# The operands of the two branch products made in two parts under attention, kept in DRAM, and only loaded in the branch stage

## The chip, the cores and the metric

The kernel runs on one core of a Trainium2 chip. The metric is the device time of one execution in microseconds (us): 3035.47 us is the median of three runs of the kernel before, which lie between 3035.05 and 3037.78. The engines are TensorE (PE), VectorE (DVE), ScalarE (ACT), GpSimd (POOL) and SyncE (SP). SP does nothing but issue transfers between DRAM and the on-chip memory; POOL issues some as well, on a queue of its own.

## The reference

One layer of a streaming encoder is computed for a prompt of 512 tokens and a sample of 64 tokens, T = 576 columns in all, with a model width of 2048. Cut to what matters here:

```python
proj = h @ w_in                                   # all projections of the layer
o_a, S_new = gated_delta_rule(q, k, v, g, beta, S0)
o_a = rmsnorm(o_a, gdn_norm_w) * silu(z_a)        # (T, 16 heads x 128)
y_a = o_a @ w_branch_a                            # first branch product, 2048 x 2048
o_b = sparse_attention(...)                       # 16 heads, top-k of the keys
y_b = (o_b * silu(z_b)) @ w_branch_b              # second branch product, 2048 x 2048
merged = sigmoid(gl_a) * y_a + sigmoid(gl_b) * y_b
x = x + gate * (merged @ w_out)                   # third product, then a last rmsnorm
```

The operand of the first branch product is called ga in the kernel (o_a times silu(z_a)), that of the second gb.

## The kernel before, in words

**Tiles.** All large products run as a stream of 189 tiles. A tile is one block of 128 columns of a weight matrix against all 2048 rows and all 576 tokens. A float32 product is made out of three reduced-precision products: the weight is split into two parts (whi, wlo) and the activation as well (hi and lo), and whi x hi, whi x lo and wlo x hi are summed. So a tile is 96 matmuls of 288 columns: 64 with whi (part 0), then 32 with wlo (part 1). `run_tile` (L314) issues them. While tile n runs, `split` (L276) makes the parts of tile n+1's weight: ACT copies four quarters of the raw weight to whi and their negative to wlo, and POOL then adds the raw weight onto wlo with two accumulating transfers. At the 84th matmul `load` lets SP fetch the raw weight of tile n+3. The same splitting of an activation is the helper `two` (L253): ACT writes the high part, DVE subtracts it to make the low part.

**Stages around the change.** Attention runs under the tiles of the query and of the gate z_b, two tiles to a head, with `attend` (L1344) for the prompt and `attend_sample` (L1397) for a pair of heads of the sample; its result is the gated tile gb of a head, stored to DRAM as `d_gb`. Before attention, the delta rule has stored its heads to `d_oa`, and silu(z_a) of heads 0 to 11 to `d_za`. Heads 12 to 15 of z_a are tiles of their own behind attention (za12 to za15, tiles 129 to 132 of the stream). Then come eight tiles of the gate of branch b (g18 to g115, tiles 133 to 140), 16 tiles of the first branch product (ya, tiles 141 to 156), 16 of the second (yb) and 16 of the output product (wo).

`open_ga` (L1789) stands in front of tile 133. It ends attention, frees its memory, lays the two parts of ga there and starts `load_ga` (L1562), which fetches half a head of d_oa and d_za at a time, multiplies on DVE and splits with `two`, in 32 steps under the eight gate tiles. `open_branch` (L1799), in front of the first ya tile, does the same for gb with `load_gb` (L1599), in 16 steps under the ya tiles.

**What sets the order.** Work beside the tiles is written as tasks (generators). After each matmul the builder looks which tasks are due by its own estimate of the engines' clocks (`tick`, L156), and has them issue their next instructions at that place of the program. That is done when the program is built. On the chip each engine works through its own list strictly in that order, and an instruction whose operand isn't there holds all that stand behind it on that engine. A stage boundary runs every task to its end before it goes on:

```python
    def drain(self):
        while self.tasks:
            self.join(*self.tasks)

    def open_ga(self):
        self.drain()
        self.c3.close()
```

`join` moves the builder's own clock on to the next due time without a matmul in between, so whatever tasks still have to issue then stands in one piece in front of the tile, on every engine's list.

Of the kernel before, what the change touches and what calls it, by code (L numbers as in the profile page):

```python
# [7 lines left out]
F32 = mybir.dt.float32  # L8
F32R = mybir.dt.float32r
I32 = mybir.dt.int32  # L10
AF = mybir.ActivationFunctionType
ALU = mybir.AluOpType
# [8 lines left out]
T = 576  # L21
# [6 lines left out]
H = 16  # L28
# [180 lines left out]
class Kern(Plan):  # L209
# [138 lines left out]
    def consts(self, ctx):  # L348
        nc, tc, i = self.nc, self.tc, self.i
        cp = self.cp = ctx.enter_context(tc.tile_pool(name="cp", bufs=1))  # L350
        self.ident = cp.tile([128, 128], F32, name="ident")
        self.A.dma_start(self.ident, i["k_ident"])
        self.mE = cp.tile([128, 2, 128], F32, name="mE")
        self.ones = cp.tile([128, 1], F32, name="ones")
        self.V.memset(self.ones, 1.0)
        self.pm = ctx.enter_context(tc.tile_pool(name="pm", bufs=3, space=PSUM))
        self.px = ctx.enter_context(tc.tile_pool(name="px", bufs=2, space=PSUM))
        self.pc = ctx.enter_context(tc.tile_pool(name="pc", bufs=2, space=PSUM))
        self.po = ctx.enter_context(tc.tile_pool(name="po", bufs=1, space=PSUM))
        self.dp = ctx.enter_context(tc.tile_pool(name="dp", bufs=1, space=DRAM))  # L360
        dt = self.dp.tile
        self.d_g = dt([16, TX], F32, name="d_g")
        self.d_kT = dt([2, 128, T], F32, name="d_kT")
        self.d_v = dt([T, 256], F32, name="d_v")
        self.d_oa = dt([H, 128, T], F32, name="d_oa")
        self.d_za = dt([H, 128, T], F32, name="d_za")
        self.d_gb = dt([H, 128, T], F32, name="d_gb")
        self.d_t = dt([2, KO, 128, T], F32, name="d_t")
        self.d_ya = dt([KO, 128, T], F32, name="d_ya")
        self.d_f = dt([16, 384], F32, name="d_f")  # L370
        self.d_F = dt([16, 128, 384], F32, name="d_F")
        self.d_D = [dt([128, T], F32, name=f"d_D{e}") for e in range(2)]
# [971 lines left out]
    def attend(self, a):  # L1344
        S, p, h = self.S, self.p3, a["h"]
        yield from self.wait(self.kv_task)
        BT = p.tile([128, 256], F32, tag="BT", name=f"BT{h}")
        S.dma_start(BT, self.toeplitz(h, 128, 256))
        yield [BT, a["qT"], a["zt"]]
        yield from self.wait(*[self.spawn(self.attend_block(a, t, BT)) for t in (3, 2, 1, 0)])  # L1350
        if h % 2:
            a["sample"] = self.spawn(self.attend_sample(h // 2))

# [43 lines left out]
    def attend_sample(self, m):  # L1397
        V, A, S, p = self.V, self.A, self.S, self.p3
        KT, KC, VV = self.kvs
        sc = 128 ** -0.5  # L1400
        at = [self.att[2 * m], self.att[2 * m + 1]]
# [7 lines left out]
        for g, (k, n, n0) in enumerate(((KC[:, 0:512], 512, 512), (KC[:, 512:1024], 512, 384), (KT[:, TP:T], 64, 0))):  # L1409
            pl = yield from self.tp(f"lgs{m}{g}")  # L1410
            self.mm(pl[:, :n], qs, k)
            a = 512 * g
# [9 lines left out]
        for g in range(3):  # L1422
            n = 4 if g < 2 else 1
# [14 lines left out]
        for s in range(2):  # L1438
            gb = at[s]["gb"]
            V.scalar_tensor_tensor(gb[:, TP:], po[:, 64 * s:64 * s + 64], 0.5, at[s]["zt"][:, TP:], op0=ALU.mult, op1=ALU.mult)  # L1440
        self.drop("po")
        yield [at[0]["gb"], at[1]["gb"]]
        for s in range(2):
            S.dma_start(self.d_gb[2 * m + s], at[s]["gb"])

    def qb_pre(self, h):
        def pre():
# [33 lines left out]
    def zb_epi(self, h):  # L1481
        def epi(ps, s):
            p, a = self.p3, self.att[h]
            if s == 0:
                a["zt"] = p.tile([128, T], F32, tag="zt", name=f"zt{h}", bufs=4)
            self.silu2(ps, s, a["zt"])
            if s == 1:
                if h >= 3:
                    t = self.att[(h - 3) | 1]
                    self.join(t["task"])  # L1490
                    self.join(t["sample"])
                a["gb"] = p.tile([128, T], F32, tag="gb", name=f"gb{h}", bufs=3)
                a["task"] = self.spawn(self.attend(a))
        return epi
# [65 lines left out]
        return epi  # L1560

    def load_ga(self):  # L1562
        units = [(h, s) for h in range(H) for s in range(2)]
        t = {}

        def load(n):
            if n < len(units):
                h, s = units[n]
                t[n] = [self.p5.tile([128, 288], F32, tag=g, name=f"{g}{n}", bufs=3) for g in ("oa", "za")]
                for x, d in zip(t[n], (self.d_oa, self.d_za)):  # L1570
                    self.S.dma_start(x, d[h][:, 288 * s:288 * s + 288])
        load(0)
        load(1)
        for n, (h, s) in enumerate(units):
            load(n + 2)
            o, z = t.pop(n)
            yield [o, z]
            self.V.tensor_tensor(o, o, z, op=ALU.mult)
            yield [o]
            sl = slice(288 * s, 288 * s + 288)  # L1580
            self.two(o, self.ga[0][:, h, sl], self.ga[1][:, h, sl])

    def ya_pre(self, j):
        def pre():
# [13 lines left out]

    def load_gb(self):  # L1599
        for h in range(H):  # L1600
            t = self.p6.tile([128, T], F32, tag="gbl", name=f"gbl{h}")
            self.S.dma_start(t, self.d_gb[h])
            yield [t]
            self.two(t, self.gb[0][:, h, :], self.gb[1][:, h, :])
            yield 4000

    def yb_pre(self, j):
        def pre():
# [170 lines left out]
    def open_att(self):  # L1779
        self.drain()  # L1780
        self.c2.close()
        self.c3, self.p3 = self.pool("p3")
        self.slack = 0.0
        self.gpool = lambda: self.p3
        self.spawn(self.conv_out())
        self.spawn(self.gate_vectors())
        self.qb_pre(0)()

    def open_ga(self):  # L1789
# [152 lines left out]
```

## Time and profile before

| | |
|---|---|
| median of three runs | 3035.47 us |
| profiled execution: time, span | 3037.4 us, 3035.6 us |
| PE, PE weight load busy | 2938.0 us (97%), 2824.9 us (93%) |
| ACT, DVE, POOL busy | 1531.8 us (50%), 1205.0 us (40%), 399.3 us (13%) |
| bytes moved | 558.84 MB, mean 184 GB/s |

The profiled execution took 3037.4 us; the span from its first to its last instruction is 3035.6 us, and all places in the trace are counted from the span's start. Busy time of PE is an overlap of pipelined matmuls, each about 300 ns long and started every 0.13 us; a stretch in which PE is busy throughout runs at the pace of its matmuls, and what is missing there is time in which PE waited.

### The profile page before, as it was taken

What the parts mean: (1) busy time and instruction counts of PE and PEld (TensorE: products, weight loads), DVE (VectorE), ACT (ScalarE), POOL (GpSimd) and SP (SyncE); (2) the same over time, 40 slices, a digit from 0 to 9 for tenths busy, and PEclk for the clock granted to TensorE, in tenths of its full rate; (3) what the DMA queues carried; (4) which work ended last, traced back from release to release, by engine and by line L of the source; (5) the groups of instructions that cost most, each with busy time, mean ns of one, the idle gap of its engine ahead of it and who ended that gap; (6) DMA issues with size and microseconds to landing.
All of it is one profiled execution on the core that took longest, in us unless ns stands there. A gap on an engine that the chain in (4) does not pass through costs nothing.

```text
span 3035.6 us, 59288 instructions
## 1 busy us (share of the span) xinstructions
PE 2938.0 (97%) x23931; PEld 2824.9 (93%) x23931; DVE 1205.0 (40%) x3643; ACT 1531.8 (50%) x3428; POOL 399.3 (13%) x792
## 2 busy tenths in 40 slices
PE   5999999999999999999999999899999999999897
PEld 2599999999999999999999999899999999999897
DVE  3344896544454455544542434244322111112112
ACT  3266445555555555655554545354544443344454
POOL 1011111111111111111111111000111111111110
PEclk7999999999999999999999999999999999999999
DMA  9875887667677666767768677777679889888875
GB/s 326 273 162 125 188 191 183 158 161 177 154 164 168 157 161 155 172 163 173 168 158 191 164 165 179 177 168 167 151 171 263 231 223 225 217 204 213 217 160 139
DMA packets 571379, 558.84 MB, mean 184 GB/s; under 512 B 55121, under 2 KB 465650, under 8 KB 569890
## 3 DMA queue, kind: packets, MB, share of 16 engines
q1 hardware_dynamic: 515794, 354.69, 40.8%
q0 software_dynamic: 55168, 200.30, 34.5%
q8 instruction: 188, 3.08, 0.4%
q14 instruction: 85, 0.70, 0.1%
q10 hardware_dynamic: 144, 0.07, 0.0%
HBM read 313.52 MB, written 47.48 MB: 119 GB/s over the span
## 4 chain that ended last, share of the span: by engine, by line
PE 82%; DMA 10%; ACT 3%; DVE 2%; SPq 2%; issue 1%; POOL 0%; ACTq 0%; DVEq 0%; POOLq 0%
PE mm L221 66%; DMA yl<-d_ya 2%; SPq L58 2%; DMA za<-d_za 2%; DMA wlo<-wraw 1%; DMA wa<-in_w_ada 1%; DMA gbl<-d_gb 1%; PE ob L221 1%; PE lg L221 1%; PE ada L221 1%; PE po L221 1%; PE mmp L221 1%; PE dot L221 1%; DMA xf<-in_x_sample 1%; ACT wlo L58 1%
## 5 line engine op out<-in xcount | busy, mean ns | idle before, releaser
L221 PE MATMUL mm<-hh,whi 128*128 128x288 f32 (+1 forms) x4448 | 1223.8, 301 | 3.9 <-ACT gth L58 3.7
L221 PE MATMUL mm<-hl,whi 128*128 128x288 f32 (+1 forms) x4448 | 1221.2, 300 | 0.0
L221 PEld LDWEIGHTS mm<-hh,whi 128*128 128x128 f32 (+1 forms) x4448 | 838.0, 188 | 13.8 <-ACT gth L58 4.2
L221 PEld LDWEIGHTS mm<-hl,whi 128*128 128x128 f32 (+1 forms) x4448 | 838.4, 188 | 8.2 <-issue 3.8
L221 PE MATMUL mm<-hh,wlo 128*128 128x288 f32 (+1 forms) x4448 | 685.1, 302 | 0.0
L221 PEld LDWEIGHTS mm<-hh,wlo 128*128 128x128 f32 (+1 forms) x4448 | 615.4, 189 | 1.9 <-issue 0.9
L58 POOL DMA_DIRECT2D wlo<-wraw x376 | 323.2, 860 | 2231.9 <-ACT wlo L58 1875.4
L58 ACT ACTIVATE whi<-wraw 128x512 fp32r<-128x512 f32 x756 | 467.3, 618 | 96.9 <-DMA wraw<-in_w_branch_b 61.0
L58 ACT ACTIVATE wlo<-whi 128x512 fp32r<-128x512 f32 x752 | 475.2, 632 | 77.2 <-PE mm L221 37.3
L221 PE MATMUL mm<-ga,whi 128*128 128x288 f32 x1024 | 141.9, 299 | 8.2 <-DVE ta L58 8.2
L221 PEld LDWEIGHTS mm<-ga,whi 128*128 128x128 f32 x1024 | 139.5, 191 | 8.9 <-DVE ta L58 8.9
L221 PE MATMUL mm<-mg,whi 128*128 128x288 f32 x1024 | 144.0, 298 | 0.0
L221 PE MATMUL mm<-gb,whi 128*128 128x288 f32 x1024 | 139.9, 296 | 0.6 <-DVE tb L58 0.6
L221 PEld LDWEIGHTS mm<-mg,whi 128*128 128x128 f32 x1024 | 138.7, 189 | 0.0
L221 PEld LDWEIGHTS mm<-gb,whi 128*128 128x128 f32 x1024 | 137.5, 188 | 1.3 <-DVE tb L58 1.3
L58 DVE SCALAR_TENSOR_TENSOR cv<-raw,cw,cv 128x579 f32<-128x579 f32 x144 | 117.9, 818 | 27.8 <-ACT cv L58 24.2
L58 DVE SCALAR_TENSOR_TENSOR gacc<-gada,cs,gacc 128x512 f32<-128x512 f32 x120 | 86.2, 744 | 3.2 <-DMA gada<-in_w_ada 3.2
L58 ACT ACTIVATE raw<-mm 128x288 f32<-128x288 f32 x96 | 36.7, 382 | 82.9 <-PE mm L221 82.1
L58 ACT ACTIVATE gth<-mm 128x288 f32<-128x288 f32 x64 | 25.9, 407 | 103.7 <-PE mm L221 102.5
L58 ACT ACTIVATE x<-px 128x128 f32<-128x128 f32 x80 | 21.9, 273 | 107.7 <-PE px L221 107.7
L58 DVE TENSOR_TENSOR xf<-yp,xf 128x512 f32<-128x512 f32 (+1 forms) x18 | 11.4, 632 | 161.7 <-PE yp L236 134.0
L58 DVE SCALAR_TENSOR_TENSOR tb<-tb,mm 128x288 f32<-128x288 f32 x32 | 14.5, 453 | 144.3 <-DMA tb<-d_t 105.1
(494 smaller groups left out, 3437.8 us busy)
## 6 DMA issues: line engine op xcount, KB each, us to landing
wlo<-wraw POOLq DMA_DIRECT2D x376, 512.0 KB, 5.4
wraw<-in_w_in SPq DMA_DIRECT2D x140, 1024.0 KB
wa<-in_w_ada SPq DMA_DIRECT2D x64, 512.0 KB
gada<-in_w_ada SPq DMA_DIRECT2D x64, 256.0 KB
wraw<-in_w_branch_a SPq DMA_DIRECT2D x16, 1024.0 KB
wraw<-in_w_branch_b SPq DMA_DIRECT2D x16, 1024.0 KB
wraw<-in_w_out SPq DMA_DIRECT2D x16, 1024.0 KB
d_t<-gth SPq DMA_DIRECT2D x32, 288.0 KB
```

What stands on the lines that cost most here:

```text
L58: r = f(*a, **k)
L221: self.nc.tensor.matmul(out, lhsT, rhs, start=start, stop=stop, **k)
```

## The change

In attention, each head's gb is now split into its two parts in three pieces of 192 columns: `part` copies the high part on ACT, subtracts on DVE and stores both with SP. Two pieces hold columns of the prompt alone, the third is made when the sample is done. A new task, `ga_parts`, started when attention begins, goes through all 16 heads in three pieces each: SP loads 192 columns of d_oa and d_za, DVE multiplies, and `part` splits and stores. Every piece, of ga or gb, goes through one pair of buffers (shi, slo), and a piece of ga through one pair of load buffers (so, sz); `part` holds the pair until 3000 ns of the builder's clock after its stores. DRAM now keeps two parts of each operand, `d_ga` and `d_gb`. In the branch stages `load_ga` and `load_gb` only load the parts into the on-chip operands, 32 transfers of 288 KB each, issued by POOL.

```diff
--- before.py
+++ after.py
@@ -364,7 +364,7 @@
         self.d_v = dt([T, 256], F32, name="d_v")
         self.d_oa = dt([H, 128, T], F32, name="d_oa")
         self.d_za = dt([H, 128, T], F32, name="d_za")
-        self.d_gb = dt([H, 128, T], F32, name="d_gb")
+        self.d_ga, self.d_gb = (dt([2, H, 128, T], F32, name=n) for n in ("d_ga", "d_gb"))
         self.d_t = dt([2, KO, 128, T], F32, name="d_t")
         self.d_ya = dt([KO, 128, T], F32, name="d_ya")
         self.d_f = dt([16, 384], F32, name="d_f")
@@ -1348,6 +1348,7 @@
         S.dma_start(BT, self.toeplitz(h, 128, 256))
         yield [BT, a["qT"], a["zt"]]
         yield from self.wait(*[self.spawn(self.attend_block(a, t, BT)) for t in (3, 2, 1, 0)])
+        a["split"] = [self.spawn(self.part(a["gb"], self.d_gb, h, s)) for s in range(2)]
         if h % 2:
             a["sample"] = self.spawn(self.attend_sample(h // 2))
 
@@ -1439,9 +1440,34 @@
             gb = at[s]["gb"]
             V.scalar_tensor_tensor(gb[:, TP:], po[:, 64 * s:64 * s + 64], 0.5, at[s]["zt"][:, TP:], op0=ALU.mult, op1=ALU.mult)
         self.drop("po")
-        yield [at[0]["gb"], at[1]["gb"]]
         for s in range(2):
-            S.dma_start(self.d_gb[2 * m + s], at[s]["gb"])
+            at[s]["split"].append(self.spawn(self.part(at[s]["gb"], self.d_gb, 2 * m + s, 2)))
+
+    def part(self, src, dst, h, s):
+
+        p, c = self.p3, slice(192 * s, 192 * s + 192)
+        yield [src]
+        yield from self.take("part")
+        hi, lo = (p.tile([128, 192], F32R, tag=n, name=f"{n}{dst.tensor.name}{h}{s}", bufs=1) for n in ("shi", "slo"))
+        self.two(src if src.shape[1] == 192 else src[:, c], hi, lo)
+        yield [hi, lo]
+        self.S.dma_start(dst[0, h][:, c], hi.bitcast(F32))
+        self.S.dma_start(dst[1, h][:, c], lo.bitcast(F32))
+        yield 3000
+        self.drop("part")
+
+    def ga_parts(self):
+
+        p = self.p3
+        for h in range(H):
+            for s in range(3):
+                o, z = (p.tile([128, 192], F32, tag=n, name=f"{n}{h}{s}", bufs=1) for n in ("so", "sz"))
+                c = slice(192 * s, 192 * s + 192)
+                self.S.dma_start(o, self.d_oa[h][:, c])
+                self.S.dma_start(z, self.d_za[h][:, c])
+                yield [o, z], 3000
+                self.V.tensor_tensor(o, o, z, op=ALU.mult)
+                yield from self.part(o, self.d_ga, h, s)
 
     def qb_pre(self, h):
         def pre():
@@ -1489,6 +1515,7 @@
                     t = self.att[(h - 3) | 1]
                     self.join(t["task"])
                     self.join(t["sample"])
+                    self.join(*self.att[h - 3]["split"])
                 a["gb"] = p.tile([128, T], F32, tag="gb", name=f"gb{h}", bufs=3)
                 a["task"] = self.spawn(self.attend(a))
         return epi
@@ -1560,25 +1587,10 @@
         return epi
 
     def load_ga(self):
-        units = [(h, s) for h in range(H) for s in range(2)]
-        t = {}
-
-        def load(n):
-            if n < len(units):
-                h, s = units[n]
-                t[n] = [self.p5.tile([128, 288], F32, tag=g, name=f"{g}{n}", bufs=3) for g in ("oa", "za")]
-                for x, d in zip(t[n], (self.d_oa, self.d_za)):
-                    self.S.dma_start(x, d[h][:, 288 * s:288 * s + 288])
-        load(0)
-        load(1)
-        for n, (h, s) in enumerate(units):
-            load(n + 2)
-            o, z = t.pop(n)
-            yield [o, z]
-            self.V.tensor_tensor(o, o, z, op=ALU.mult)
-            yield [o]
-            sl = slice(288 * s, 288 * s + 288)
-            self.two(o, self.ga[0][:, h, sl], self.ga[1][:, h, sl])
+        for h in range(H):
+            for s in range(2):
+                self.G.dma_start(self.ga[s][:, h, :], self.d_ga[s, h])
+            yield 2000
 
     def ya_pre(self, j):
         def pre():
@@ -1598,11 +1610,9 @@
 
     def load_gb(self):
         for h in range(H):
-            t = self.p6.tile([128, T], F32, tag="gbl", name=f"gbl{h}")
-            self.S.dma_start(t, self.d_gb[h])
-            yield [t]
-            self.two(t, self.gb[0][:, h, :], self.gb[1][:, h, :])
-            yield 4000
+            for s in range(2):
+                self.G.dma_start(self.gb[s][:, h, :], self.d_gb[s, h])
+            yield 8000
 
     def yb_pre(self, j):
         def pre():
@@ -1784,6 +1794,7 @@
         self.gpool = lambda: self.p3
         self.spawn(self.conv_out())
         self.spawn(self.gate_vectors())
+        self.spawn(self.ga_parts())
         self.qb_pre(0)()
 
     def open_ga(self):
```

How the change moves instructions is shown at two places of the program. The first is the boundary between tile 132 (za15) and the gate tiles. On ACT, before, the four quarters of the weight of tile 134 stand right behind the two copies that end za15; whi and wlo are the parts of a weight, gz is z_a's gate, mm a tile's sum, gth a gate tile's result, and the number behind a name is the tile's or the head's:

```order
L58 ACTIVATE gz15_26606<-mm132_0_26511 128x288
L58 ACTIVATE gz15_26606<-mm132_1_26554 128x288
L58 ACTIVATE whi134_26657<-wraw134_26495 128x512
L58 ACTIVATE wlo134_26658<-whi134_26657 128x512
...
L58 ACTIVATE wlo134_26658<-whi134_26657 128x512
L58 ACTIVATE ga0_26635<-oa0_26642 128x288
L58 ACTIVATE gth18_26754<-mm133_0_26640 128x288
```

On ACT now (shid_ga_84 is the buffer of a high part of ga; the digits behind it are the head and the piece, so 110 is head 11, piece 0):

```order
L58 ACTIVATE gz15_27235<-mm132_0_27128 128x288
L58 ACTIVATE gz15_27235<-mm132_1_27181 128x288
L58 ACTIVATE shid_ga_84102_27259<-so102_27167 128x192
L58 ACTIVATE shid_ga_84110_27271<-so110_27266 128x192
L58 ACTIVATE shid_ga_84111_27282<-so111_27277 128x192
...
L58 ACTIVATE shid_ga_84151_27414<-so151_27409 128x192
L58 ACTIVATE shid_ga_84152_27425<-so152_27420 128x192
L58 ACTIVATE whi134_27448<-wraw134_27108 128x512
L58 ACTIVATE wlo134_27449<-whi134_27448 128x512
...
L58 ACTIVATE gth18_27545<-mm133_0_27441 128x288
```

Sixteen copies of ga pieces (head 10's last, then heads 11 to 15 with three each) now stand between za15 and the weight of tile 134; the ten rows left out are pieces of heads 12 to 14 and the rest of heads 11 and 15, and the other gap holds six more quarters of the weight.

On SP, at the same place, before (oa and za are the halves of a head that load_ga fetches):

```order
L58 DMA wraw135_26613<-in_w_in 128x16x128
L58 DMA d_za_83<-gz15_26606 128x576
L58 DMA oa0_26642<-d_oa_82 128x288
L58 DMA za0_26643<-d_za_83 128x288
L58 DMA oa1_26646<-d_oa_82 128x288
L58 DMA za1_26647<-d_za_83 128x288
...
L58 DMA wraw136_26767<-in_w_in 128x16x128
```

On SP now (so and sz are the loads of a ga piece, d_ga its stores, wraw a raw weight):

```order
L58 DMA wraw135_27242<-in_w_in 128x16x128
L58 DMA d_za_83<-gz15_27235 128x576
L58 DMA d_ga_84<-shid_ga_84102_27259 128x192
L58 DMA d_ga_84<-slod_ga_84102_27260 128x192
L58 DMA so110_27266<-d_oa_82 128x192
L58 DMA sz110_27267<-d_za_83 128x192
L58 DMA d_ga_84<-shid_ga_84110_27271 128x192
L58 DMA d_ga_84<-slod_ga_84110_27272 128x192
L58 DMA so111_27277<-d_oa_82 128x192
...
L58 DMA d_ga_84<-slod_ga_84152_27426 128x192
L58 DMA wraw136_27551<-in_w_in 128x16x128
```

Each piece of ga is four rows in a fixed order, load, load, store, store. The fetch of the raw weight of tile 136 stood behind five pairs of loads, and now stands behind all pieces up to head 15.

The second place is POOL's list under the gate tiles. Before, it holds the two accumulating transfers of each tile's weight and nothing else:

```order
L58 DMA wlo133_26517<-wraw133_26343 128x1024 x2
L58 DMA wlo134_26658<-wraw134_26495 128x1024 x2
L58 DMA wlo135_26788<-wraw135_26613 128x1024 x2
L58 DMA wlo136_26939<-wraw136_26767 128x1024 x2
L58 DMA wlo137_27090<-wraw137_26911 128x1024 x2
```

Now (ga0 and ga1 are the high and low parts of the operand, a row for each head):

```order
L58 DMA wlo133_27136<-wraw133_26929 128x1024 x2
L58 DMA ga0_27436<-d_ga_84 128x576
L58 DMA ga1_27437<-d_ga_84 128x576
L58 DMA wlo134_27449<-wraw134_27108 128x1024
L58 DMA ga0_27436<-d_ga_84 128x576
L58 DMA ga1_27437<-d_ga_84 128x576
L58 DMA wlo134_27449<-wraw134_27108 128x1024
...
L58 DMA wlo135_27574<-wraw135_27242 128x1024
...
L58 DMA wlo137_27826<-wraw137_27679 128x1024 x2
```

Four loads stand in front of the end of wlo134; between it and wlo135 stand ten, then two between wlo135's halves; and all 32 stand in front of wlo137.

## Rows read from the trace of the kernel before

**Rows 1.** The page, part 1: busy us (share of the span) xinstructions:

```profile
PE 2938.0 (97%) x23931; PEld 2824.9 (93%) x23931; DVE 1205.0 (40%) x3643; ACT 1531.8 (50%) x3428; POOL 399.3 (13%) x792
```

**Rows 2.** Stretches: start:end, us, busy by engine, PEclk, DMA share, GB/s:

```profile
1619.00:2250.00 631.00, 617.03 (x4474) 590.11 (x4474) 238.52 (x716) 306.09 (x649) 63.76 (x74) 0.99 0.72 170
2250.00:2374.00 124.00, 120.31 (x901) 119.84 (x900) 30.28 (x68) 58.53 (x119) 13.77 (x16) 1.00 0.94 241
2374.00:2590.00 216.00, 207.81 (x1543) 207.13 (x1542) 24.48 (x47) 88.21 (x152) 29.30 (x34) 0.98 0.93 229
```

**Rows 3.** Waits of TensorE, 2250 to 2374: us, times, longest:

```profile
PE mm L221 <- ACT gth L58: 3.7, 2, 2.3
```

**Rows 4.** Waits of TensorE, 2374 to 2590:

```profile
PE mm L221 <- DVE ta L58: 8.2, 3, 4.8
```

**Rows 5.** Instructions on ga: ns min/median/max, first and last start:

```profile
L58 ACT ACTIVATE ga<-oa x32: 426/444/447, 2275.1 to 2370.6; 128x288 fp32r<-128x288 f32 x32
L58 DVE TENSOR_TENSOR ga<-oa,ga x32: 457/458/460, 2275.6 to 2371.1; 128x288 fp32r<-128x288 f32 x32
```

**Rows 6.** Instructions on gbl:

```profile
L58 ACT ACTIVATE gb<-gbl x16: 668/684/687, 2394.4 to 2542.5; 128x576 fp32r<-128x576 f32 x16
L58 DVE TENSOR_TENSOR gb<-gbl,gb x16: 751/758/759, 2395.1 to 2543.2; 128x576 fp32r<-128x576 f32 x16
```

**Rows 7.** The page, part 3: queue, packets, MB, share of 16 engines:

```profile
q1 hardware_dynamic: 515794, 354.69, 40.8%
q0 software_dynamic: 55168, 200.30, 34.5%
```

**Rows 8.** Timeline of DVE, 2265 to 2284:

```profile
2268.41 0.45 DVE L58 SCALAR_TENSOR_TENSOR gz<-gz,mm 128x288 f32<-128x288 f32 x1 [1.68 <-ACT gz L58]
2274.62 0.46 DVE L58 TENSOR_TENSOR oa<-oa,za 128x288 f32<-128x288 f32 x1 [5.76 <-DMA za<-d_za]
2275.59 0.46 DVE L58 TENSOR_TENSOR ga<-oa,ga 128x288 fp32r<-128x288 f32 x1 [0.51 <-ACT ga L58]
```

**Rows 9.** Timeline of SP, 2223 to 2300 (issues):

```profile
2269.26 0.42 SPq L58 DMA_DIRECT2D oa<-d_oa  x1
2269.73 0.49 SPq L58 DMA_DIRECT2D za<-d_za  x1
2276.08 0.32 SPq L58 DMA_DIRECT2D oa<-d_oa  x1
```

**Rows 10.** Timeline of SP and DVE, 610 to 613:

```profile
610.24 1.04 SPq L58 DMA_DIRECT2D M<-dN  x3
612.79 0.17 DVE L58 TENSOR_TENSOR Mt<-M 36x14 f32<-36x14 f32 x1 [1.88 <-DMA M<-dN]
```

**Rows 11.** Timeline of ACT, 2266 to 2281:

```profile
2267.96 0.41 ACT L58 ACTIVATE gz<-mm 128x288 f32<-128x288 f32 x1 [1.73 <-PE mm L221]
2268.27 0.62 ACT L58 ACTIVATE whi<-wraw 128x512 fp32r<-128x512 f32 x1
2275.11 0.45 ACT L58 ACTIVATE ga<-oa 128x288 fp32r<-128x288 f32 x1 [2.00 <-DVE oa L58]
```

**Rows 12.** Timeline of PE, 2258 to 2281: start, us, operation:

```profile
2263.50 4.43 PE L221 MATMUL mm<-hh,wlo 128*128 128x288 f32 x32
2267.76 0.30 PE L221 MATMUL mm<-hh,whi 128*128 128x288 f32 x1
2280.56 0.30 PE L221 MATMUL mm<-hh,whi 128*128 128x288 f32 x1
```

**Rows 13.** The stretch behind a stop of TensorE:

```profile
2396.00:2400.00 4.00, 3.73 (x18) 3.74 (x19) 0.58 (x2) 3.69 (x7) 0.86 (x1) 0.59 1.12 349
```

**Rows 14.** Chain of waits, 2360 to 2385: start, us, piece:

```profile
by line: DMA za<-d_za 35.1%; DMA d_t<-gth 23.0%; SPq L58 15.9%; ACT wlo L58 12.7%; ACT whi L58 8.4%; ACT gth L58 3.7%; issue 3.4%; DVE ga L58 1.9%; DVE oa L58 1.9%; ACT ga L58 1.6%; DVEq L58 0.1%; ACTq L58 0.1%
```

**Rows 15.** Timeline of POOL, 2272 to 2300:

```profile
2273.40 0.86 POOL L58 DMA_DIRECT2D wlo<-wraw  x1 [1.51 <-ACT wlo L58]
```

## Prediction

> **What bounds the kernel now.** I read the page first: TensorE is busy for 97% of the span and no other engine for more than 50% [rows 1], so an edit changes the time only where TensorE stops or starts to run. Then the stretches around the change [rows 2]. TensorE is idle for 631.0 - 617.0 = 14.0 us under attention, 124.0 - 120.3 = 3.7 us under the gate tiles, 216.0 - 207.8 = 8.2 us under the first branch product. The waits name the causes: 3.7 us for ACT to empty a gate tile [rows 3] and 8.2 us for DVE to finish a branch tile [rows 4]. These 11.9 us, and some time at half clock behind the stops, are all that the edit in the branch stages can win. The last thing to see is the transfer share there, 0.94 and 0.93: the 16 transfer engines are nearly full, against 0.72 under attention.
>
> **What is removed.** Under the gate tiles ACT loses 32 copies of 444 ns and DVE 64 instructions of 457 ns (32 products, 32 subtractions) [rows 5]; under ya ACT loses 16 of 684 ns and DVE 16 of 758 ns [rows 6]. Both engines have room in those stretches (ACT 58.5 of 124 us), so the gain is only that these instructions no longer stand in front of those TensorE waits for: at best the 3.7 and the 8.2 us and some 1.7 us of clock (4 us at 0.59 [rows 13]).
>
> **What is added under attention.** From the rows of 288 and 576 columns a DVE instruction costs (758 - 457)/288 = 1.05 ns a column more, so 192 columns take 457 - 96 x 1.05 = 357 ns; likewise ACT 364 ns [rows 5, 6]. 96 pieces add 96 x 0.364 = 35 us to ACT and (96 + 48) x 0.357 = 51 us to DVE, which are busy 306 and 239 of 631 us. The transfers grow by 48 x 2 loads and 96 x 2 stores of 98 KB less the 4.7 MB stored to d_gb before, 23.6 MB, of which 5.9 MB fall behind the stretch (below). At the 286 GB/s that SP's queue makes (354.69 MB in 0.408 x 3035.6 us) [rows 7] that is 62 us, or a share of 0.72 + 0.10 = 0.82. What is the cost? Stretches with 0.93 to 0.94 idle by 3% and 4% [rows 2], which in 631 us would be 19 to 25 us in place of 14; at 0.82 I take +4 us, between 0 and +11.
>
> **What is left over.** This is the term that decides. The order shows that the ga pieces don't come to an end under attention: when za15 is through, head 10's last piece and all of heads 11 to 15 are still to be issued, and the stage boundary issues them in one block. On ACT the block stands in front of the split of tile 134's weight, which TensorE needs as soon as it has done tile 133. The 15 pieces run strictly one behind the other: SP must wait for the low part before it issues its store, and the next piece's two loads stand behind that store; the product waits for the loads, the copy for the product, the subtraction for the copy. One piece costs:
> - Issue. SP starts 0.03 us after DVE's end (2275.59 + 0.46 to 2276.08) and issues one transfer in 0.47 us (2269.26 to 2269.73) [rows 8, 9]; store and first load in front of the second load make 0.9 us.
> - Landing of the second load. No row has a 98 KB load in a quiet stretch. The lower end: three 8 KB loads were issued from 610.24 to 611.28 and the waiting DVE instruction began at 612.79 [rows 10], 1.85 us after the last began; 197 KB more at 286 GB/s add 0.7: 2.5 us. The upper end: za, issued at 2269.73 in a full stretch, released DVE at 2274.62 [rows 8, 9]: 4.9 us. In the block nothing else is fetched, since the next raw weight stands behind it on SP and the loads of ga wait for the freed memory, so I go with the lower end, and 0.3 us for the 98 KB store just ahead in the queue: 2.8 us.
> - Product, copy, subtraction. In the row of 288 columns from 2274.62 through ACT's 2275.11 to 2276.05, 1.43 us [rows 8, 11]; three times 0.09 us less for 192 columns: 1.17 us.
>
> Together 4.87 us, times 15 is 73 us; the first piece still meets tile 135's weight in flight and takes the 4.9 us landing, +2.1. The block starts when head 10's last low part is made, 0.4 us behind the second gz on DVE (2268.41 + 0.45 + 0.4 = 2269.3) [rows 8]. It ends for ACT 0.4 us before the last subtraction does, at 2269.3 + 75.1 - 0.4 = 2344.0; the first quarter of whi takes 0.65 us more (0.62 and its release) [rows 11]. TensorE began tile 133 at 2267.76 and would begin tile 134 at 2280.56 [rows 12]. It stands for 2344.7 - 2280.6 = 64 us. With the two ends of the landing the piece costs 4.57 to 6.97 us and TensorE stands for 60 to 94 us.
>
> After such a stop the clock is lower: behind the longest stop under ya, 4.8 us [rows 4], the granted clock was 0.59 over the next 4 us [rows 13], which is mostly the lower level of 1.2 GHz and costs about 2 us. The new stop is longer; I add 2.5 us (0 to 5).
>
> A rule speaks for a longer block. The trace shows a store to DRAM that landed 5.75 us after its issue in a full stretch [rows 14]. The Trainium skill, DMA: Bandwidth & Descriptors, section Anatomy of one DMA, puts the fixed part of a transfer at about 2.0 us and most of that at the receipt of the write, longest for DRAM. By it the store of a high part would land 2.2 us after its issue, an estimate from that page, in time for the next copy, which comes over 4 us later; no run here shows a quiet store. With the row's 5.75 us instead, the next copy would wait for the store, and a piece would cost 5.75 + 0.36 + 0.05 = 6.2 us.
>
> **What the loads cost.** The 32 loads can start when the block is done, and POOL's list puts them around the weights of tiles 134 to 136. TensorE's need up to the middle of wlo137 is three tiles of 12.8 us [rows 12], 64 matmuls of part 0 (8.5 us) and 1 us: 48 us. In that time must land 9.4 MB of loads and 3.1 MB of raw weights and 1.2 MB of stores at 286 GB/s (48 us), and 4.2 MB of accumulating transfers at the 191 GB/s of POOL's queue (200.30 MB in 0.345 x 3035.6 us), 22 us [rows 7]. That is 70 us, or with 2 us to the first landing 72: TensorE waits for 24 us. Ends: 3.7 us, what the same bytes cost before when they were spread [rows 3]; and if loads on POOL's queue run at its 191 GB/s too, 88 - 48 = 40 us. The issue itself, 40 times 0.86 us [rows 15], is less than 48 us and hidden. I keep 24, the row of the fuller queue being near the middle. Under ya the loads of gb bring 4.7 MB more than before, 54 MB at 256 GB/s (241/0.94) [rows 2] is 212 us in a stretch whose tiles need 16 x 12.8 = 205 and that took 216: -3 us (-10 to +5).
>
> **Sum.** +64 + 2.5 + 24 - 3.7 (the old wait under the gates) + 4 - 3 = +88 us on the profiled execution's 3037.4 us, 3125; the median of the runs is 1.9 us lower, so 3123 us.
>
> **Rivals.**
> 1. The pieces pace at the landing of a full stretch (loads of 4.9 us, or stores). For it: the load of za that released DVE in a full stretch is like this [rows 8, 9]. Against: those shared the engines with weights and with loads issued ahead of need. TensorE stands 94 us, +30: 3152 us.
> 2. The loads are hidden as they are before, and the branch stage gives back all: +64 + 2.5 - 3.7 - 8.2 - 1.7 = +53, 3088 us. For it: raw weights are two tiles ahead. Against: 32 loads stand ahead of wlo137 in one queue.
> 3. Not slower: the block is hidden behind tile 133, and the branch waits go, -3.7 - 8.2 - 1.7: 3022 us. The block would have to fit in the 12.8 us of tile 133 [rows 12], 0.85 us a piece, which means that a piece's loads come before the stores of the one ahead. Against: SP's order, and ACT's, in which the weight of tile 134 comes behind all pieces. Above (12.8 + 13.6)/15 = 1.8 us a piece even that case, with the loads at no cost, is slower than before.
>
> **How the numbers follow.** My forecast 0.70, rival 1 0.13, rival 2 0.12, rival 3 0.04, and 0.01 for an attention stretch that idles by more than its bound. The range reaches from just under rival 2 to just over rival 1, 3085 to 3158, which also holds the ends of the landing and of the loads' rate taken singly. 0.2%, 6 us, is about what a measurement of this kernel can tell from no change: faster 0.03, within 0.01, slower 0.96.
>
> **What would show it.** One idle stretch of TensorE of 60 us or more behind the first gate tile, released by ACT's whi, with DVE doing triples of short instructions 4.9 us apart; a clock near half behind it; TensorE waiting for POOL's wlo at the next two or three tiles; few waits later in the gates. Wrong would be a block that is over within some 15 us, a spacing of 7 us, or a loss that lies under attention.

## The result

The changed kernel takes 3114.93 us (median of four runs, 3107.86 to 3121.03), the kernel before 3036.62 us in the same session: a ratio of 1.0244, with a 95% interval of 1.0225 to 1.0264. The change costs 78 us. The profile was taken in the slowest of the four, 3121.03 us with a span of 3119.3; it is compared with the profile before at 3035.6, so it has 83.7 us to account for.

### The profile page after: what moved, and what is told of

Its sections match the earlier page's. It is cut to its first block, busy times and chain, and to the rows that moved or that the text cites. A ratio compares the mean times of both kernels' runs of the same rounds, so it can differ in the third digit from the quotient of the medians.

```text
span 3119.3 us, 59930 instructions
## 1 busy us (share of the span) xinstructions
PE 2947.0 (94%) x23931; PEld 2831.4 (91%) x23931; DVE 1209.0 (39%) x3707; ACT 1538.6 (49%) x3476; POOL 435.1 (14%) x856
## 4 chain that ended last, share of the span: by engine, by line
PE 81%; DMA 12%; ACT 2%; DVE 2%; SPq 1%; issue 1%; POOL 0%; ACTq 0%; DVEq 0%; POOLq 0%
PE mm L221 67%; DMA wlo<-wraw 2%; SPq L58 1%; DMA d_t<-gth 1%; PE ob L221 1%; DMA sz<-d_za 1%; PE po L221 1%; PE mmp L221 1%; PE dot L221 1%; PE ada L221 1%; DMA xf<-in_x_sample 1%; DMA ta<-d_t 1%; PE lg L221 1%; DMA wraw<-in_w_branch_a 1%; ACT whi L58 1%
## 5 line engine op out<-in xcount | busy, mean ns | idle before, releaser
L221 PE MATMUL mm<-hh,whi 128*128 128x288 f32 (+1 forms) x4448 | 1225.5, 301 | 74.9 <-ACT whi L58 58.5
L221 PEld LDWEIGHTS mm<-hh,whi 128*128 128x128 f32 (+1 forms) x4448 | 841.1, 189 | 84.9 <-ACT whi L58 58.8
L58 ACT ACTIVATE wlo<-whi 128x512 fp32r<-128x512 f32 x752 | 475.2, 632 | 93.1 <-PE mm L221 61.3
L58 DVE SCALAR_TENSOR_TENSOR ta<-ta,mm 128x288 f32<-128x288 f32 x32 | 13.9, 453 | 313.9 <-PE mm L221 173.3
L58 ACT ACTIVATE x<-px 128x128 f32<-128x128 f32 x80 | 21.9, 274 | 108.2 <-PE px L221 108.1
```

The source lines that it names most:

```text
L58: r = f(*a, **k)
L221: self.nc.tensor.matmul(out, lhsT, rhs, start=start, stop=stop, **k)
```

## The profile after

First the page: busy time by engine (to be set beside [rows 1]), and the slices of the span for TensorE and its granted clock.

```profile
PE 2947.0 (94%) x23931; PEld 2831.4 (91%) x23931; DVE 1209.0 (39%) x3707; ACT 1538.6 (49%) x3476; POOL 435.1 (14%) x856
...
PE   5999999999999999999999999999936999999897
...
PEclk8999999999999999999999999999967999999999
```

TensorE's 97% have become 94%, with a hole of two slices (78 us each) at the place of the gate tiles. The stretches show the same ([rows 2]; columns: stretch, its length, busy time of PE, PEld, DVE, ACT and POOL, clock, transfer share, GB/s):

```profile
1619.00:2250.00 631.00, 615.45 (x4468) 588.32 (x4467) 269.14 (x822) 324.99 (x723) 62.79 (x73) 0.99 0.80 197
2250.00:2374.00 124.00, 58.79 (x409) 57.80 (x407) 14.71 (x42) 25.91 (x55) 18.14 (x31) 0.73 0.58 153
2374.00:2460.00 86.00, 74.75 (x549) 74.75 (x550) 0.00 (x0) 33.14 (x63) 15.87 (x23) 0.92 0.95 234
2460.00:2676.00 216.00, 207.96 (x1556) 207.27 (x1555) 13.91 (x32) 78.71 (x134) 46.13 (x65) 0.99 0.97 244
```

Under attention TensorE idles for 15.6 us of 631, hardly more than before (14.0), and under the first branch product (from 2460) for 8.0 of 216, as before (8.2). The loss lies between. The waits of TensorE from 2250 to 2460 ([rows 3]; total, times, longest):

```profile
PE mm L221 <- ACT whi L58: 58.5, 1, 58.5
PE mm L221 <- ACT gth L58: 16.1, 1, 16.1
PE mm L221 <- DMA wlo<-wraw: 1.8, 1, 1.8
```

and from 2460 to 2680, under ya, a wait of the same name and size as before ([rows 4]):

```profile
PE mm L221 <- DVE ta L58: 8.0, 3, 5.8
```

The stop of 58.5 us is the block of left-over pieces. The chain of waits shows how one follows the other (start, duration, what; SPq is SP issuing a transfer, the DMA line the time until that transfer landed):

```profile
2278.87 4.32 DMA sz<-d_za
...
2283.75 0.37 ACT shid_ga L58
2284.14 0.32 SPq L58
...
2284.56 0.38 SPq L58
...
2284.99 0.44 SPq L58
...
2285.52 1.98 DMA sz<-d_za
...
2287.62 0.37 DVE so L58
2288.06 0.37 ACT shid_ga L58
...
2289.79 2.09 DMA sz<-d_za
...
2292.44 0.37 ACT shid_ga L58
```

One copy of ACT (shid_ga) follows the other at 2283.75, 2288.06 and 2292.44, 4.3 to 4.4 us apart: two stores and a load issued, the second load landed in 2.0 to 2.1 us (2.0 to 2.2 over the whole block), product, copy. The subtraction adds next to nothing: DVE ended it at 2284.51, when SP had just issued the store of the high part, and the store of the low part was issued at 2284.56.

Farther on the same view shows the end of the block and the second wait:

```profile
2345.04 0.37 ACT shid_ga L58
...
2345.85 1.68 DMA d_ga<-slod_ga
...
2350.82 9.03 DMA wlo<-wraw
...
2359.98 0.38 SPq L58
...
2360.42 24.28 DMA d_t<-gth
...
2384.78 0.42 ACT gth L58
```

ACT has finished the gate tile's result, gth, at 2350.7. Its store stands behind a raw weight on SP, and SP waits 13.6 us before it can issue that weight at 2359.98: the buffer is free only when POOL's accumulating transfer of an earlier weight has landed, the 9.03 us from 2350.82. Then the store takes 24.28 us to land, counted from the start of its issue, which alone holds SP for 10.51 us; before, the slow one took 5.75 [rows 14]. gth has one buffer there, so ACT can't empty the next gate tile until 2384.78, and TensorE finds no free accumulator. POOL issues 11 of the 32 ga loads between 2348 and 2360, around that accumulating transfer, and 15 more in the 25 us in which the store lands.

From tile to tile: tile 133 starts at 2274.5 instead of 2267.8 [rows 12], 6.7 us late. But 5.5 of these were there before the change touches anything: tile 95, the last to start before SP issues the first load of a ga piece (1632.91), starts at 1624.75 instead of 1619.22. First the row of the kernel before, then two of the changed kernel, from the timelines of PE and SP:

```profile
1619.22 0.30 PE L221 MATMUL mm<-hh,whi 128*128 128x288 f32 x1
```

```profile
1624.75 0.30 PE L221 MATMUL mm<-hh,whi 128*128 128x288 f32 x1
...
1632.91 1.27 SPq L58 DMA_DIRECT2D so<-d_oa  x1
```

So attention, from tile 95 to tile 133, takes 649.7 us instead of 648.5, 1.2 us more; three runs below with the same attention (e3, e6 and e7) take 650.6 to 653.2. From tile 133 to the first ya tile it takes 184.9 us instead of 106.6: 72.7 us more of waits (58.5 + 16.1 + 1.8 - 3.7) and the clock behind the two stops:

```profile
2346.00:2351.00 5.00, 5.00 (x21) 5.00 (x22) 0.00 (x0) 4.90 (x10) 2.86 (x6) 0.50 0.44 124
2351.00:2356.00 5.00, 5.00 (x39) 5.00 (x39) 0.00 (x0) 4.34 (x8) 3.30 (x6) 1.00 1.10 231
2385.00:2390.00 5.00, 4.75 (x24) 4.75 (x25) 0.00 (x0) 4.87 (x10) 1.84 (x3) 0.65 1.06 303
```

5 us at 0.50 and 5 us at 0.65 cost 2.5 + 1.8 = 4.3 us. The stage of ya takes 213.6 us instead of 215.4.

## The experiments

Theory A was that the loss is the serial block, the burst of ga loads behind it, and a few us under attention. The rivals are that the added pieces and bytes cost the same wherever they stand, and, for the second wait, that the transfers are late whatever their spacing or queue. Each time below is a median beside the kernel before on the same chip. "Gates" is the time from the start of tile 133 to the first ya tile in the profiled execution, "stop" and "gth" are TensorE's waits there for ACT's whi (the longest) and gth. The small "stop" of e8 and e10 doesn't stand behind the first gate tile, but behind a later one.

| run | us | ratio to before, 95% | gates | stop | gth |
|---|---|---|---|---|---|
| before | 3036.62 | | 106.6 | none | 3.7 |
| after | 3114.93 | 1.0225 to 1.0264 | 184.9 | 58.5 | 16.1 |
| e0, order of z_a | 3039.56 | 0.9993 to 1.0017 | 113.1 | none | 8.3 |
| e1, gb alone | 3037.64 | 0.9989 to 1.0011 | 112.1 | none | 7.0 |
| e2, ga alone | 3062.26 | 1.0069 to 1.0111 | 144.0 | 16.1 | 16.3 |
| longer hold | 3135.77 | 1.0303 to 1.0344 | 211.6 | 83.6 | 16.8 |
| e4, no block | 3071.70 | 1.0093 to 1.0135 | 118.6 | none | 13.2 |
| e5, no block, spread | 3067.20 | 1.0089 to 1.0119 | 117.5 | none | 10.9 |
| e3, spread | 3111.75 | 1.0232 to 1.0262 | 183.2 | 58.8 | 15.1 |
| e6, two gth | 3108.57 | 1.0210 to 1.0258 | 176.4 | 57.7 | none |
| e7, loads by SP | 3112.08 | 1.0222 to 1.0268 | 184.0 | 59.7 | 10.4 |
| e8, ga alone, no block | 3034.44 | 0.9982 to 1.0006 | 108.2 | 3.9 | none |
| e10, loads only | 3038.62 | 0.9995 to 1.0014 | 107.8 | 3.5 | none |

**One half at a time.** The run with gb alone keeps the old `load_ga` and starts no ga pieces:

```diff
-        self.spawn(self.ga_parts())
```

> Only gb is made in parts under attention and loaded by POOL; ga is loaded, multiplied and split in the branch stage as before, so there are no ga pieces and nothing is left over at the boundary. Theory A (the loss is the block of 15 left-over ga pieces in front of tile 134, 58.5 us, the burst of ga loads behind it, 16 to 18 us, and some 5 us under attention): no stop of TensorE of more than 6 us at the gates, time 3036 to 3042 us. Theory B (the loss is the price of the added pieces and of their 23.6 MB, wherever they stand; gb has 48 of the 96 pieces and a third or more of the bytes): 30 to 45 us slower than before, 3065 to 3080 us.

3037.64 us, no difference. 48 pieces under attention and 16 double loads under ya cost nothing that can be measured, and win nothing. Theory B, a price for each piece wherever it stands, falls.

The run with ga alone stores gb whole and splits it under ya as before, and has z_a's last heads earlier:

```diff
-            z(1) if h % 4 else gate(1)
+            z(1)
...
-        z(len(zs))
+        gate(4)
```

> Only ga is made in parts under attention; gb is stored whole and split under ya as before. The pair of buffers then serves ga alone, and z_a's last heads are computed ahead of attention's end, so that 5 pieces are left over at the boundary instead of 15. Theory A (4.4 us for each left-over piece, less the 7 us that tile 133 covers): a stop of 15 us behind the first gate tile, at most 18 us for the burst of ga loads, 3 us under attention; 3053 to 3072 us. Theory B (price of the pieces and their bytes, of which ga has the larger part): 3078 us or more.

3062.26 us, within A's range. Its waits from 2250 to 2420:

```profile
PE mm L221 <- ACT gth L58: 16.3, 1, 16.3
PE mm L221 <- ACT whi L58: 16.1, 1, 16.1
```

With 5 left-over pieces the stop is 16.1 us, with 15 it is 58.5: 4.24 us for each.

**More left-over pieces.** The work is the same, but a piece holds the shared buffers longer:

```diff
-        yield 3000
+        yield 4500
         self.drop("part")
```

> As the changed kernel, but a piece holds its pair of buffers for 4500 ns of the builder's clock instead of 3000, so that 21 ga pieces are left over in the block instead of 15; work and bytes are the same. Theory A (4.4 us for each left-over piece): the stop behind the first gate tile is 58.5 + 6 x 4.4 = 85 us, 3139 to 3145 us, perhaps a few us less where attention is relieved. Theory B (the stop is something of the boundary itself, the same however many pieces it holds): 3112 to 3118 us.

3135.77 us, under A's 3139 to 3145, which allowed for a few us less. The waits from 2250 to 2480:

```profile
PE mm L221 <- ACT whi L58: 83.6, 1, 83.6
PE mm L221 <- ACT gth L58: 16.8, 1, 16.8
```

83.6 - 58.5 = 25.1 us for six pieces more, 4.18 each. The three stops (5, 15, 21 pieces) lie on one line. The time rises by less, 21 us, since attention is shorter with fewer pieces in it: 641.5 us from tile 95 to tile 133 instead of 649.7.

**No block at all.** z_a's last heads come earlier, as in the run with ga alone, and a ga piece is split inside its own load buffers, without the pair that gb uses:

```diff
-                yield [o, z], 3000
+                yield [o, z], 1000
...
-                yield from self.part(o, self.d_ga, h, s)
+                yield [o]
+                hi = z.bitcast(F32R)
+                self.A.activation(hi, o, AF.Copy)
+                yield [z]
+                self.V.tensor_tensor(o.bitcast(F32R), o, z, op=ALU.subtract)
+                yield [o]
+                self.S.dma_start(self.d_ga[0, h][:, c], z)
+                self.S.dma_start(self.d_ga[1, h][:, c], o)
+                yield 1500
```

> As the changed kernel, with all 96 pieces and all bytes, but the 48 ga pieces all come to an end before the boundary: z_a's last heads are computed ahead of attention's end, and a ga piece is split inside its own load buffers, without waiting for the pair that gb uses. Theory A: no stop of 58 us behind the first gate tile; what is left is the burst of loads, 0 to 18 us, and 5 to 10 us under attention: 3040 to 3062 us. Theory B (the price of the pieces and the bytes): attention is longer by what the block took, 3090 us or more.

3071.70 us: the stop is gone, but neither theory's range holds the time. The loss is now under attention, where tile 133 starts at 2296.2 against 2270.8 in the control below. TensorE, DVE and SP waited there (1619 to 2296) for:

```profile
PE lg L221 <- DVE L L58: 13.2, 5, 7.5
...
DVE so L58 <- DMA sz<-d_za: 33.7, 12, 10.7
DVE L L58 <- DMA BT<-d_F: 31.0, 5, 12.0
...
SPq L58 <- DMA d_ga<-so: 111.1, 38, 9.5
```

Read from the last line up: SP stands for 111 us because the next piece's load may not overwrite a buffer before the store out of it has landed; attention's table BT is issued behind that on SP, and DVE needs it for the logits L that TensorE multiplies next. So this edit put a new wait where attention needs SP. Whether the loss is due to this form of the pieces, or comes with all 96 of them under attention, isn't settled: the run with ga alone and a later one, e8, lose nothing there, but they have only the 48 pieces of ga. No run has all 96 there in another form.

The control of z_a's order, the kernel before with the two lines of the first diff of e2 alone:

> A control: the kernel before, with only the one thing done to it that the runs with fewer left-over pieces share, namely that z_a's last four heads are computed in the delta rule's stage and four gate tiles behind attention in their place. All theories: no change, 3036 us within 5. If it is faster or slower by more, the runs with ga alone or without a block have to be compared with this one.

3039.56 us, no change.

**The second wait.** Four runs were to tell whether the 16.1 us come from the spacing of the loads, the one buffer of gth, POOL's queue, or the bytes. The loads further apart:

```diff
                 self.G.dma_start(self.ga[s][:, h, :], self.d_ga[s, h])
-            yield 2000
+            yield 5000
```

> As the changed kernel, but the 32 loads of ga are spread over six to seven gate tiles instead of three (5000 ns of the builder's clock between heads instead of 2000). Theory A (the second wait under the gates, 16.1 us at ACT's gth, comes from the burst of loads, behind which one store of gth takes 24 us to land): the block's 58.5 us stay, the 16 us go, 3098 to 3103 us. Rival (that wait comes from the late start behind the block, with raw weights and stores queued up by SP, whatever the loads' spacing): no change, 3115 us. Second rival (loads that come late are missed by the first tile of ya): a new wait at the first ya tile of 5 to 20 us.

3111.75 us. A expected 3098 to 3103 and was wrong; the first rival, no change, is nearest. The one wait became three (2260 to 2460), with the transfer share at 0.99 from 2341 to 2453:

```profile
PE mm L221 <- ACT whi L58: 58.8, 1, 58.8
PE mm L221 <- ACT gth L58: 15.1, 3, 10.2
PE mm L221 <- DMA wlo<-wraw: 1.2, 1, 1.2
...
2341.00:2453.00 112.00, 95.51 (x676) 94.58 (x676) 0.00 (x0) 41.65 (x78) 31.63 (x48) 0.92 0.99 242
```

During the block only the pieces' own transfers run (91 GB/s from 2284 to 2345 in the changed kernel), and the loads that before had eight tiles have seven.

Two buffers for gth:

```diff
-                n = 2 if p is self.p2 else 1
+                n = 2 if p in (self.p2, getattr(self, "p5", None)) else 1
```

> As the changed kernel, but gth, the result of a gate tile, has two buffers instead of one under the gate tiles. The block of 58.5 us stays in every theory. Theory A (the 16.1 us at ACT's gth are the wait for its one buffer, whose store takes 24 us to land behind a raw weight; the transfers themselves are not late): 8 to 16 us faster, 3099 to 3107 us, no wait at gth over 5 us. Theory B (the 16 transfer engines are full and everything that has to land in that stretch is late): the wait moves to the weights (whi or wlo) or to the next gth, 3111 to 3118 us.

3108.57 us, between the two theories. No wait for gth is left, but weights come late in its place (2260 to 2460; 61.3 - 57.7 = 3.6 us for whi beside the block):

```profile
PE mm L221 <- ACT whi L58: 61.3, 2, 57.7
PE mm L221 <- DMA wlo<-wraw: 6.9, 4, 2.6
```

10.5 us of 17.9 are left. By this pair of profiles taking away the one buffer is worth 7 us of the wait, and late weights make the rest; the intervals of the times don't tell this run from the changed kernel.

The loads issued by SP:

```diff
-                self.G.dma_start(self.ga[s][:, h, :], self.d_ga[s, h])
+                self.S.dma_start(self.ga[s][:, h, :].bitcast(F32), self.d_ga[s, h])
```

> As the changed kernel, but the 32 loads of ga are issued by SP instead of POOL; the block of 58.5 us stays. Theory A (the queue of POOL is what is slow: its loads and the accumulating transfers of the weights' low parts share it and hold back raw weights and stores): the 16 us under the gates shrink by 8 or more, 3098 to 3107 us. Theory B (the bytes are what takes the time, whatever the queue): 3110 to 3118 us. Rival (a load that waits in SP's order holds back the raw weight behind it): 3118 us or more, with TensorE waiting for ACT's whi.

3112.08 us, so B: the queue doesn't decide it. Waits for gth of 10.4 us and for wlo of 2.7 are left.

Then the run without a block, with the loads 5000 ns apart in place of 2000:

> The run without a block (all 96 pieces, all under attention), with the loads of ga spread as well (5000 ns of the builder's clock between heads instead of 2000). There the eight gate tiles have their whole time for the loads. Theory A (with 125 us for them the bytes fit, and only their bunching made the wait of 13.2 us): that wait shrinks by 8 or more, 3059 to 3066 us; the 28 us under attention stay. Theory B (the transfer engines are full there in any case): 3069 to 3076 us.

3067.20 us, in the gap between the two ranges. Its wait for gth is 10.9 us in three pieces instead of 13.2 in one, so the spacing alone isn't it here either. Tile 133 starts at 2295.9, so the loss under attention stayed.

**The ga half without its costs.** From the run with ga alone, with shorter dues, so that no piece is left over, two buffers of gth, and 4000 ns between the loads:

```diff
-        yield 3000
+        yield 1000
         self.drop("part")
...
-                yield [o, z], 3000
+                yield [o, z], 2000
```

> As the run with ga alone in parts, but the pieces are due sooner (2000 ns of the builder's clock for the loads instead of 3000, 1000 ns of hold instead of 3000), so that none is left over at the boundary; gth has two buffers, and the loads are spread over some five gate tiles. Theory A (left-over pieces, one buffer of gth and the burst are all that the ga half costs): no stop behind the first gate tile and no wait at gth over 5 us, 3030 to 3042 us. Theory B (pieces that are pressed into attention cost there what they cost in the block; the run without a block lost 28 us there): attention longer by 10 to 25 us, 3045 to 3062 us.

3034.44 us, as A expected and no more than before: the ratio's interval includes 1. The stop and the wait for gth are gone; tile 133 starts at 2269.9, against 2270.8 in the control. The transfer share from 2250 to 2374 is 1.00, against 0.95 from 2374 to 2460 in the changed kernel, so full transfer engines alone don't make a long wait here. From 2250 to 2600 TensorE waits for

```profile
PE mm L221 <- DVE ta L58: 5.2, 3, 3.0
PE mm L221 <- ACT whi L58: 3.9, 1, 3.9
```

**What there was to win.** The kernel before with nothing added under attention; whole heads of d_oa, d_za and d_gb are loaded in place of the parts, and product and split are left out:

```diff
+        for h in range(H):
+            for s, d in enumerate((self.d_oa, self.d_za)):
+                self.G.dma_start(self.ga[s][:, h, :], d[h])
+            yield 4000
...
+            for s in range(2):
+                self.G.dma_start(self.gb[s][:, h, :], self.d_gb[h])
+            yield 8000
```

> What the branch stages could win at best: the kernel before, with nothing added under attention, in which the branch stages load whole heads of d_oa and d_za in place of the two parts of ga, and each head of d_gb twice in place of the two parts of gb (so the product, the split and the parts are left out), 32 transfers each by POOL, those of ga spread over five gate tiles, gth with two buffers. Theory A (the branch stages are held by the 16 transfer engines, which the loads fill as before; ACT and DVE were not what held them): 3029 to 3040 us, no gain over 0.25%. Theory B (the old splits stood in the way of the tiles, and their 11.9 us of waits come back): 3022 to 3028 us.

3038.62 us, no gain, with ACT and DVE freed of all of it. The stretches of [rows 2] and TensorE's waits from 2250 to 2600:

```profile
2250.00:2374.00 124.00, 120.47 (x892) 120.15 (x891) 1.82 (x4) 49.34 (x92) 33.81 (x51) 0.99 1.00 243
2374.00:2590.00 216.00, 203.64 (x1503) 202.72 (x1503) 13.10 (x30) 75.48 (x128) 45.09 (x63) 0.97 0.96 242
...
PE mm L221 <- DVE ta L58: 11.8, 3, 7.8
PE mm L221 <- ACT whi L58: 3.5, 1, 3.5
```

DVE has dropped to 1.82 us under the gates, and the transfers have come to a share of 1.00. With 0.5 us for a wlo TensorE waits for 15.8 us instead of the old 11.9; the control e0, whose branch stages are those of before, waits for 13.7 (8.3 at gth, 5.4 at ta).

The waits for ta look alike and have another cause. ta is a gate that SP loads from d_t, and DVE multiplies it by the sum of a ya tile. The chain in front of the longest of these waits, in the kernel before and then in this run:

```profile
2386.92 7.43 DMA gbl<-d_gb
...
2394.38 0.69 ACT gb L58
...
2395.77 0.46 DVE ta L58
```

```profile
2395.95 14.39 DMA ta<-d_t
...
2410.44 0.47 DVE ta L58
```

Before, all three of these waits run through the split: DVE stands in its order at the subtraction of gb, which waits for ACT's copy and that for the landing of gbl (7.4 to 11.6 us). Here the split is gone, and all three run through the landing of ta itself, issued right behind a raw weight on SP (14.1 to 16.2 us). In the changed kernel the longest does too (14.79 us). So the old waits did go, and new ones came that are no shorter. Loads issued in another way, or each head of gb loaded once, weren't run; what such a kernel would win is open.

## Why the prediction was right, and where its terms were off

- **The block: right, 58.5 us against 64.** 15 pieces were left, as the order said, one behind the other, released by ACT's whi. The term that was mis-sized is the landing of the second load: from its issue to the product 2.8 us were taken, 2.1 to 2.4 measured, 2.2 on average. The rest of a piece took 2.2 us against 2.07 (1.4 from ACT's end to the issue of the second load, in which the subtraction is hidden, and 0.8 for product and copy). The piece measures 4.4 us, not 4.87, under the lower end of 4.57. The first landing was foreseen at 4.9 and took 4.32. Part of this was made up by a term that the sum left out: in front of the first piece SP had the store of d_za and both stores of head 10 to issue, so its second load was issued 3.0 us after head 10's last subtraction (2275.86 to 2278.87), not 0.9.
- **The rule on stores: no longer block.** The Trainium skill, DMA: Bandwidth & Descriptors, section Anatomy of one DMA, puts the fixed cost of a transfer at about 2 us, most of it in the receipt of the write. It gives that for transfers that GpSimd issues, and these stores are SP's. By the rule the store was in time, and the trace agrees: the quiet store of the last low part landed in 1.68 us, and no next copy waited for a store. The 2.2 us that were estimated from the page for a store would also have been nearer to the loads' landing (2.0 to 2.2) than the 2.8 taken.
- **The clock: 2.5 us right for the first stop** (0.50 over 5 us). The second stop, foreseen as waits at three tiles, cost 1.8 more.
- **The loads: 17.9 us against 24 (3.7 to 40), in the wrong place.** That the number lies in the range is luck. The step that failed is "TensorE waiting for POOL's wlo at the next two or three tiles". The sum counted what has to land before wlo137 and took POOL's queue for the late one. In the run TensorE waited 16.1 us for ACT's gth and only 1.8 for wlo: the store of gth was late, behind a raw weight on SP, which in its turn had waited for a wlo of POOL. No single cause of this was found: taking away the one buffer, the close spacing or POOL's queue, each alone, left 10.5 to 16.3 us. Nor do full transfer engines make it alone: e8, with two buffers, wider spacing and no block, filled them and waited for 3.9 us.
- **What was to come back: -6.7 foreseen, -5.5 in the profiles.** The old 3.7 us under the gates are gone, but with the new waits in their place; ya's stage gained 1.8 for the 3 taken, with its wait at 8.0 us instead of 8.2. The loads-only run shows why: the splits did stand in front of that wait, but with them gone ta's own load comes late, and 11.8 us are waited for it. The sentence that the 11.9 us "are all that the edit in the branch stages can win" was an upper bound, and with these loads nothing of it is won.
- **Attention: +4 foreseen, 1.2 us in the profiled pair,** within 0 to 11, and 2.1 to 4.6 in the three other runs with the same attention. Each half by itself took 643.4 us (gb) and 650.6 (ga, in e8) from tile 95 to tile 133, against 648.5 before and 648.2 in the control. So the term is about as large as the difference between profiles, and whether the two halves add up to more isn't settled.

Together: 5.5 us that lie before the first changed instruction, and 1.2 + 72.7 + 4.3 - 1.8 = 76.4 behind it, make 81.9 of the 83.7 us between the profiles. Between the medians it is 78.3, against 88 predicted: the block and the loads came out 5.5 and 6.1 us shorter than foreseen and attention 2.8, while the clock cost 1.8 more and ya gave back 1.2 less. The rivals fell: the pieces didn't pace at a full stretch's landing, the loads weren't hidden, and the block was not behind tile 133.

What two buffers of gth alone would do without a block stays open. The run of ga alone without a block has them and spaced loads together and waits for 3.9 us; the run without a block that has the spacing alone waits for 10.9, with more pieces under attention.

## What to carry to other kernels

Count what tasks still have to issue at a boundary that runs them to their end: there they come one behind the other at their full latency, here 4.2 to 4.4 us a piece, however cheap they are beside other work. Before moving work off an engine, run the kernel with that work left out and its new loads put in: here it would have shown no gain, since the waits that the work made were replaced by waits, no shorter, for late transfers. And when loads are bunched into a full stretch, look at the stores that share its queue and have one buffer.

## What was unexpected of the hardware

- A transfer of 288 KB issued right behind one of 1 MB on SP's queue landed in 24.28 us while POOL issued loads; its issue alone held SP for 10.51 us. In the kernel before, one of the same stage took 5.75 [rows 14]. Loads of ta, of the same size and in the same place behind a raw weight, took 14.1 to 16.2 us in the loads-only run.
- With the ga loads on SP instead of POOL the transfer engines moved more at less of their time, in the same stretch as the spread run's row above: 245 / 0.93 works out to 263 GB/s at a full share, against 242 / 0.99 = 244. That is one profile of each, and it didn't shorten the kernel.

```profile
2341.00:2453.00 112.00, 97.19 (x664) 96.25 (x665) 0.71 (x2) 42.81 (x80) 13.77 (x16) 0.91 0.93 245
```
